# Issuing the samples' state and value-row loads from SyncE instead of GpSimd

## The chip, the cores and the metric

The kernel runs on one core of a Trainium2 chip. The metric is the device time in microseconds of one execution, from launch to the last output. Times of a kernel are given as the median of several runs. A profiled execution has a span, from its first to its last recorded instruction, and a time of its own that is a little longer.

In the text PE is TensorE, DVE is VectorE, ACT is ScalarE, POOL is GpSimd and SP is SyncE. L1077 is line 1077 of the kernel.

## What is computed

The reference is one inference step of a decoder layer with three parallel token mixers, for a prompt of 256 tokens and for 8 samples of one token each. Cut to what matters here:

```python
z = h @ w_in                                   # (tokens, 15376), split into the branches' inputs
# A: gMLP spatial gating   B: HGRN2, 8 heads of 128 x 128   C: GLA, 4 heads of 128 x 256
S_t = diag(f_t) @ S_{t-1} + outer(k_t, v_t)    # B and C, per head
o_t = S_t.T @ q_t
merged = sum(sigmoid(z_gate[n]) * (branch[n] @ w_branch[n]) for n in range(3))
x = x + gt1 * rmsnorm(merged @ w_out)
x = x + gt2 * rmsnorm(relu(h2 @ w_mlp_up) ** 2 @ w_mlp_down)
```

The prompt starts from zero states. Each sample has states of its own, given as inputs (`state_hgrn`, `state_gla`), and returns them after one update: the old state is scaled by f per row, and the outer product of the sample's k and v is added. All weights are float32.

## The kernel before

All weight matrices are streamed through PE in items of 512 KB. For each item SP issues a load into one of four `raw` buffers (L616, or L609 in the first stage). ACT then rounds the item to its high part `whi` (L109), DVE takes the difference as its low part `wlo` (L106), half an item at a time, and PE multiplies three products, whi by the high part of the activations (L659), whi by their low part (L660) and wlo by their high part (L661). `Stream.ahead` issues loads five items ahead (`LOAD_AHEAD`) and splits two items ahead (`SPLIT_AHEAD`). Six half-item buffers hold `whi` and `wlo`. Each call of `linear` runs the items of 256 output columns, and after every item it calls `background`, which moves all other work on by a little.

That other work is written as Python generators. `mixer_r` does the prompts' part of one group of four heads, `samples_r` the samples' part. There are three groups: two of HGRN2 (128 x 128 states) and one of GLA (128 x 256 states). The samples' part goes in steps of 256 KB of states: for HGRN2 one sample with its four heads is a step, 8 steps for a group; for GLA two heads of a sample, 16 steps. So there are 32 steps in all. For each step:

- `fetch` loads the step's states from the input into one of four `st` buffers (`ST_BUFS`), L1077;
- `values` loads the step's value rows, broadcast to all 128 partitions, into one of two `vbc` buffers (`VB_BUFS`), L1083. The rows come from a small DRAM tensor `vs_d` that `mixer_r` wrote before (L1134);
- ACT scales the states in place by f (L1103), DVE adds k times the row (L1105), one instruction for each head;
- the new states are stored to the output by POOL (L1106);
- later `slot` has PE multiply all states of a sample with its q (L686), and the result is gathered on DVE.

The states are fetched two steps ahead and the rows one step ahead. A fetch is made only when at most one state buffer still waits for PE (L1096), and a step's update comes three calls of `background` after its fetch (`FETCHED`). An `st` buffer comes free when PE has read it and its store is done, a `vbc` buffer when DVE has made the updates of its step.

The order of the instructions on an engine is set in one of two ways. Within a `manual_schedule` block the listed engines run in program order. All other engines are ordered by the scheduler, which puts an instruction where its inputs and buffers are ready by its own estimate, earlier program lines first. From L969 to L1404, which holds all of the samples' work, the listed engines are PE and POOL. SP, ACT and DVE are ordered by the scheduler there. In the first stage (up to L844) SP too runs in program order. Whatever its origin, the order is fixed when the program is built: on the chip an engine takes its instructions one after the other, and one that waits holds up all that stand behind it.

POOL's order around the samples' work is therefore, for each step n: the state load of step n+2 (L1077), the row load of step n+1 (L1083), the store of step n (L1106). SP has the weight items and the loads of `w_ada` (L339), which the adaLN modulation needs.

Of the kernel before, what the change touches and what calls it, by code (L numbers as in the profile page):

```python
# [15 lines left out]
P = 128  # L16
# [41 lines left out]
def hybrid_step_kernel(  # L58
# [8 lines left out]
    nc = tc.nc  # L67
# [18 lines left out]
    def blk(shape=None, dt=F32):  # L86
        shape = shape or [P, 4, NT]
        return blkp.tile(shape, dt, tag="b", name=nm("b"))
# [4 lines left out]
    def tmp(shape, tag, bufs=2):  # L93
        return tp.tile(shape, F32, tag=tag, name=nm(tag), bufs=bufs)
# [4 lines left out]
    def mul(o, a, b):  # L99
        V.tensor_tensor(o, a, b, op=ALU.mult)  # L100
# [106 lines left out]
    def rstd_small(ms, scale, out):  # L207

        n, w = out.shape
        xx, aa = tmp([P, 16], "sx")[0:n, 0:w], tmp([P, 16], "sa")[0:n, 0:w]  # L210
        c = 0
        for m in ms if isinstance(ms, list) else [ms]:
            V.tensor_scalar(xx[:, c:c + m.shape[1]], m, scale, EPS, ALU.mult, ALU.add)
            c += m.shape[1]
        V.tensor_scalar(out.bitcast(I32), xx.bitcast(I32), -0.5, 1597463007.0, ALU.mult, ALU.add)
        for _ in range(3):
            mul(aa, out, out)
            V.scalar_tensor_tensor(aa, aa, -0.5, xx, ALU.mult, ALU.mult)
            V.scalar_tensor_tensor(out, aa, 1.5, out, ALU.add, ALU.mult)
# [768 lines left out]
    vs_d = dp.tile([3, 8 * NS, P], F32, tag="vs_d", name="vs_d")  # L988
# [73 lines left out]
    def samples_r(G):  # L1062

        dv = G.dv
        nj, nh = dv // P, 512 // dv
        q, k, g = G.q, G.k, G.g
        fs = tmp([P, 4, NS], "fs")
        S.activation(fs, g[:, :, NP:NT], AF.Exp)
        qm = blk([P, 4, NS, 32])
        mul(qm, q[:, :, NP:NT].unsqueeze(3).to_broadcast([P, 4, NS, 32]),  # L1070
            delta.rearrange("p (b c) -> p b c", b=NS).unsqueeze(1).to_broadcast([P, 4, NS, 32]))
        steps = [(b, h) for b in range(NS) for h in range(0, 4, nh)]
        ahead, vals = [], []

        def fetch(b, h):
            st = tmp([P, nh, dv], "st", ST_BUFS)
            nc.gpsimd.dma_start(st, G.s_in(b, h, nh))  # L1077
            ahead.append((st, now[0]))

        def values(b, h):  # L1080
            v = tmp([P, 4, P], "vbc", VB_BUFS)
            r0 = 4 * nj * b + h * nj
            nc.gpsimd.dma_start(v, vs_d[G.i, r0:r0 + 4, :].partition_broadcast(P))  # L1083
            vals.append((v.rearrange("p (h j) v -> p h (j v)", h=nh), now[0]))

        for s in steps[0:2]:
            fetch(*s)
            yield
        values(*steps[0])
        yield  # L1090
        os_ = tmp([P, dv], f"os{G.i}", 1)
        sts = []
        for n, (b, h0) in enumerate(steps):
            if n + 2 < len(steps):

                yield lambda: len(sts) + sum(len(x[3]) for x in samples) <= ST_BUFS - 3  # L1096
                fetch(*steps[n + 2])
            if n + 1 < len(steps):
                values(*steps[n + 1])
            yield lambda: now[0] >= max(ahead[0][1] + FETCHED, vals[0][1] + FETCHED - 1)  # L1100
            st, v = ahead.pop(0)[0], vals.pop(0)[0]
            for i in range(nh):
                S.activation(st[:, i, :], st[:, i, :], AF.Copy, scale=fs[:, h0 + i, b:b + 1])  # L1103
            for i in range(nh):
                V.scalar_tensor_tensor(st[:, i, :], v[:, i, :], k[:, h0 + i, NP + b:NP + b + 1], st[:, i, :], ALU.mult, ALU.add)  # L1105
            nc.gpsimd.dma_start(G.s_out(b, h0, nh), st)  # L1106
            sts.append(st)
            if h0 + nh == 4:
                samples.append((now[0], (G, qm, os_), b, sts))
                sts = []  # L1110
            yield
        yield lambda: not samples
        yield READY
        ss, rr = tmp([P, 1], "sss", 1), tmp([P, 1], "srr", 1)
        S.activation(tmp([P, dv], "vt"), os_, AF.Square, accum_out=ss)
        rstd_small(ss, 1.0 / dv, rr)
        S.activation(os_, os_, AF.Copy, scale=rr)
        G.os = os_
        yield
# [641 lines left out]
```

## Time and profile before

| | |
|---|---|
| median of 3 runs | 1835.34 us (1832.19 to 1837.56) |
| profiled execution, its own time | 1832.18 us |
| its span | 1830.4 us |
| mean granted clock of PE | 0.997 |
| DMA, mean over the span | 242 GB/s |

The page gives the busy time of each engine, the span in slices, the chain that ended last and the costliest groups of instructions. Further views are of one stretch alone: the busy time of each engine in it, who waited for whom in it, and the instructions of one engine in order of time. In the last the columns are start, duration, engine, line, operation, written and read tile, count, and in brackets the idle time before it and what ended it. In a group's row the count is followed by the busy time and the mean duration in ns, then by the idle time of the engine before these instructions. In a waits row the numbers are microseconds in total, times, and the longest. A DMA row ends with the size of one transfer and the median time from issue to landing.

### The profile page before, as it was taken

The page shows a single profiled execution, that of the slowest core. Times are in us where ns is not written, and L with a number is a line of the kernel's source. Part 1 is how long each engine was busy: PE and PEld are TensorE (multiplying, and loading weights), DVE is VectorE, ACT ScalarE, POOL GpSimd, SP SyncE. Part 2 cuts the span into 40 slices and gives each one's busy share as a digit, 9 for nine tenths or more (in the row PEclk, how much of TensorE's full clock was granted, in tenths as well). Part 3 has the DMA queues.
Part 4 walks back from the last instruction along what each step waited for, and adds up shares of the span by engine and source line. Part 5 has one row for each costly group of instructions (what it writes and reads, how often), then busy time and mean ns, then how long its engine had stood idle before and what let it go on. Part 6 is the DMA issues. An engine that isn't in the chain of part 4 may idle for free.

```text
span 1830.4 us, 42186 instructions
## 1 busy us (share of the span) xinstructions
PE 1788.7 (98%) x17012; PEld 1696.5 (93%) x17012; DVE 1181.8 (65%) x2092; ACT 1000.3 (55%) x1818; POOL 131.3 (7%) x210
## 2 busy tenths in 40 slices
PE   6999999999999999999999999999999999999998
PEld 4889999989988999989999989999999999999997
DVE  4566677787576696566555667555666666666666
ACT  5544364666755765654445666555554545454544
POOL 4221000111111101210000000000000000000000
PEclk9999999999999999999999999999999999999999
DMA  9999697788787788897987964777666666666663
GB/s 326 354 343 304 195 304 231 215 266 276 239 287 233 229 270 278 274 323 250 308 254 265 327 180 146 246 256 227 191 197 194 197 194 196 195 195 196 196 196 106
DMA packets 330179, 442.05 MB, mean 242 GB/s; under 512 B 14946, under 2 KB 276944, under 8 KB 329984
## 3 DMA queue, kind: packets, MB, share of 16 engines
q1 hardware_dynamic: 311728, 380.26, 65.0%
q0 software_dynamic: 17184, 57.85, 9.1%
q8 instruction: 133, 2.18, 0.5%
q10 hardware_dynamic: 1072, 1.25, 0.2%
q14 instruction: 62, 0.51, 0.1%
HBM read 427.60 MB, written 11.70 MB: 240 GB/s over the span
## 4 chain that ended last, share of the span: by engine, by line
PE 88%; DMA 2%; DVE 2%; issue 1%; ACT 1%; POOL 0%; DVEq 0%; ACTq 0%; POOLq 0%
PE mm L659 27%; PE mm L661 26%; PE mm L660 26%; PE ada L376 3%; DMA vbc<-vs_d 1%; PE ada L308 1%; DVE wlo L106 1%; PE sm L851 1%; PE sm L1208 1%; PE sm L679 1%; PE sm L686 1%; DMA raw<-in_w_in_dram 0%; DVE b L106 0%; PE sm L1578 0%; ACT whi L109 0%
## 5 line engine op out<-in xcount | busy, mean ns | idle before, releaser
L659 PE MATMUL mm<-b,whi 128*128 128x264 f32 x4624 | 1292.4, 279 | 12.3 <-issue 5.1
L661 PE MATMUL mm<-b,wlo 128*128 128x264 f32 x4624 | 1279.7, 277 | 5.1 <-DVE wlo L106 4.5
L660 PE MATMUL mm<-b,whi 128*128 128x264 f32 x4624 | 1278.8, 277 | 0.8 <-DVE b L106 0.7
L106 DVE TENSOR_TENSOR wlo<-raw,whi 128x512 fp32r<-128x512 f32 x1136 | 774.4, 689 | 489.1 <-ACT whi L109 475.0
L109 ACT CAST whi<-raw 128x512 fp32r<-128x512 f32 x1136 | 691.8, 616 | 644.5 <-DVE wlo L106 331.7
L659 PEld LDWEIGHTS mm<-b,whi 128*128 128x128 f32 x4624 | 875.8, 189 | 53.0 <-issue 28.0
L661 PEld LDWEIGHTS mm<-b,wlo 128*128 128x128 f32 x4624 | 876.2, 189 | 7.3 <-DVE wlo L106 7.2
L660 PEld LDWEIGHTS mm<-b,whi 128*128 128x128 f32 x4624 | 876.2, 189 | 4.4 <-issue 3.0
L103 DVE TENSOR_TENSOR b<-b,mm 128x528 f32<-128x528 f32 (+1 forms) x137 | 95.7, 699 | 24.5 <-PE mm L661 13.0
L1105 DVE SCALAR_TENSOR_TENSOR st<-vbc,b,st 128x128 f32<-128x128 f32 (+1 forms) x96 | 34.2, 390 | 55.2 <-DMA vbc<-vs_d 50.4
L1103 ACT ACTIVATE st<-st,fs 128x128 f32<-128x128 f32 (+1 forms) x96 | 37.1, 430 | 50.5 <-DMA st<-in_state_hgrn_dram 26.9
L488 POOL DMA_DIRECT2D b<-in_w_ada_dram x64 | 46.2, 724 | 126.0 <-PE ada L308 94.4
L376 PE MATMUL ada<-araw,cT 128*32 128x512 f32 x296 | 39.8, 601 | 0.0
L308 PE MATMUL ada<-b,cT 128*32 128x256 f32 (+1 forms) x640 | 35.1, 356 | 2.8 <-DMA b<-in_w_ada_dram 2.6
L100 DVE TENSOR_TENSOR b<-b,b 128x512 f32<-128x512 f32 (+1 forms) x47 | 33.9, 741 | 1.3 <-ACT b L1221 1.0
L1106 POOL DMA_DIRECT2D out_dram<-st x32 | 23.6, 736 | 130.5 <-DVE st L1105 130.5
L308 PEld LDWEIGHTS ada<-b,cT 128*32 128x32 f32 x640 | 17.8, 113 | 14.9 <-DMA b<-in_w_ada_dram 6.2
L376 PE MATMUL ada<-b,cT 128*32 128x512 f32 x216 | 26.2, 594 | 0.0
L106 DVE TENSOR_TENSOR b<-gt,b 128x528 fp32r<-128x528 f32 x32 | 22.7, 710 | 3.2
L106 DVE TENSOR_TENSOR b<-b 128x1024 f32<-128x1024 f32 (+1 forms) x24 | 24.3, 1017 | 0.0
L1632 ACT ACTIVATE b<-vt 128x528 fp32r<-128x528 f32 x32 | 23.0, 719 | 1.0
L106 DVE TENSOR_TENSOR b<-b,b 128x1056 fp32r<-128x1056 f32 (+3 forms) x21 | 20.8, 991 | 4.0 <-ACT b L109 3.8
(344 smaller groups left out, 854.0 us busy)
## 6 DMA issues: line engine op xcount, KB each, us to landing
raw<-in_w_in_dram SPq DMA_DIRECT2D x231, 512.0 KB, 4.8
raw<-in_w_mlp_up_dram SPq DMA_DIRECT2D x128, 512.0 KB, 3.9
raw<-in_w_mlp_down_dram SPq DMA_DIRECT2D x128, 512.0 KB, 3.7
araw<-in_w_ada_dram SPq DMA_DIRECT2D x74, 512.0 KB, 5.7
b<-in_w_ada_dram SPq DMA_DIRECT2D x54, 512.0 KB, 6.6
b<-in_w_ada_dram POOLq DMA_DIRECT2D x48, 512.0 KB, 8.9
raw<-in_w_branch_dram SPq DMA_DIRECT2D x48, 512.0 KB, 4.5
raw<-in_w_out_dram SPq DMA_DIRECT2D x32, 512.0 KB, 5.3
```

What stands on the lines that cost most here:

```text
L100: V.tensor_tensor(o, a, b, op=ALU.mult)
L103: V.tensor_tensor(o, a, b, op=ALU.add)
L106: V.tensor_tensor(o, a, b, op=ALU.subtract)
L109: S.copy(hi, src)
L308: T.matmul(acc[32 * j:32 * j + 32, 0:n], cT[:, k, :], w[:, n * j:n * j + n], start=k == 0, stop=k == KT - 1)
L376: T.matmul(self.acc[32 * j:32 * j + 32, :], cT[:, k, :], ws[j // 2][:, j % 2 * 512:j % 2 * 512 + 512], start=k == 0, stop=k == KT - 1)
L488: queue.dma_start(w[:, i], w1[k * P:(k + 1) * P, :, self.k0 * P:(self.k0 + self.n) * P])
L659: T.matmul(o, a, xh(k + j), start=first and j == 0, stop=False)
L660: T.matmul(o, a, xl(k + j), start=False, stop=False)
L661: T.matmul(o, b, xh(k + j), start=False, stop=last and j == n - 1)
L1103: S.activation(st[:, i, :], st[:, i, :], AF.Copy, scale=fs[:, h0 + i, b:b + 1])
L1105: V.scalar_tensor_tensor(st[:, i, :], v[:, i, :], k[:, h0 + i, NP + b:NP + b + 1], st[:, i, :], ALU.mult, ALU.add)
```

## The change

The two loads of the samples' part are issued by SP. They use the same buffers, sources and consumers as before; the stores of the new states (L1106) and the write of `vs_d` (L1134) remain on POOL.

```diff
         def fetch(b, h):
             st = tmp([P, nh, dv], "st", ST_BUFS)
-            nc.gpsimd.dma_start(st, G.s_in(b, h, nh))
+            nc.sync.dma_start(st, G.s_in(b, h, nh))
             ahead.append((st, now[0]))
 
         def values(b, h):
             v = tmp([P, 4, P], "vbc", VB_BUFS)
             r0 = 4 * nj * b + h * nj
-            nc.gpsimd.dma_start(v, vs_d[G.i, r0:r0 + 4, :].partition_broadcast(P))
+            nc.sync.dma_start(v, vs_d[G.i, r0:r0 + 4, :].partition_broadcast(P))
             vals.append((v.rearrange("p (h j) v -> p h (j v)", h=nh), now[0]))
```

## The prediction

> **What bounds the kernel now.** I read the page's busy shares first, then one window for each part of the program, then who waited for whom where the moved loads run.
>
> ```profile
> span 1830.4 us, 42186 instructions
> PE 1788.7 (98%) x17012; PEld 1696.5 (93%) x17012; DVE 1181.8 (65%) x2092; ACT 1000.3 (55%) x1818; POOL 131.3 (7%) x210
> ...
> 0.00:350.00 350.00, 329.20 (x3139) 299.41 (x3140) 228.14 (x449) 168.97 (x288) 53.81 (x85) 1.00 0.85 289
> 350.00:830.00 480.00, 469.42 (x5152) 435.71 (x5151) 335.44 (x634) 312.45 (x637) 70.31 (x106) 0.99 0.81 266
> 830.00:1830.40 1000.40, 990.07 (x8726) 961.35 (x8724) 618.18 (x1010) 518.92 (x895) 7.17 (x19) 1.00 0.68 213
> ```
>
> TensorE sets the time. In a window row the columns are length, then busy time of PE, PEld, DVE, ACT and POOL, then clock, DMA share and GB/s. The moved loads belong to 350 to 830 us, where PE is busy 469.42 of 480.00 us: it loses 10.6 us there, and no better placing of these loads can win more than that in their own stretch. The waits of that stretch say what the 10.6 us are:
>
> ```profile
> PE mm L659 <- issue: 5.1, 2, 2.9
> PE mm L661 <- DVE wlo L106: 4.3, 5, 2.3
> PE mm L659 <- ACT whi L109: 0.3, 1, 0.3
> ...
> DVE st L1105 <- DMA vbc<-vs_d: 50.4, 19, 7.4
> ...
> ACT st L1103 <- DMA st<-in_state_hgrn_dram: 26.9, 7, 7.2
> ...
> ACT st L1103 <- DMA st<-in_state_gla_dram: 16.9, 9, 3.5
> ...
> POOL st L1077 <- PE sm L686: 153.4, 11, 30.4
> POOL out_dram L1106 <- DVE st L1105: 130.5, 17, 28.2
> ```
>
> 4.3 + 0.3 = 4.6 us of PE's loss is a wait for split weights (whi, wlo), which ScalarE and VectorE make; 5.1 us has no releaser that the profile knows. VectorE stands 50.4 us, 19 times, before the state update of line 1105 until a value row (vbc) lands, and everything behind it on VectorE, the splits too, stands with it. Why the rows are late is in GpSimd's order. First GpSimd, then VectorE, at one such place:
>
> ```profile
> 764.50 0.71 POOL L1106 DMA_DIRECT2D out_dram<-st  x1 [3.52 <-DVE st L1105]
> 773.71 0.72 POOL L1077 DMA_DIRECT2D st<-in_state_gla_dram  x1 [8.49 <-PE sm L686]
> 774.43 0.57 POOL L1083 DMA_DIRECT2D vbc<-vs_d  x1
> ...
> 763.73 0.48 DVE L1105 SCALAR_TENSOR_TENSOR st<-vbc,b,st 128x256 f32<-128x256 f32 x1
> ...
> 781.87 0.88 DVE L1105 SCALAR_TENSOR_TENSOR st<-vbc,b,st 128x256 f32<-128x256 f32 x2 [7.36 <-DMA vbc<-vs_d]
> ```
>
> There are two vbc buffers. The one that is loaded at 774.43 was free when the update two steps earlier ended, at 763.73 + 0.48 = 764.2. The load went out 10.2 us later, because in program order it stands behind a state load that waits until PE has read a state buffer (8.49 us here). VectorE then waited 7.36 us.
>
> **The change, part by part.** 32 state loads and 32 row loads, 256 KB each, leave GpSimd's queue for SyncE's. Data, buffers and consumers stay.
>
> ```profile
> L1083 POOL DMA_DIRECT2D vbc<-vs_d x32 | 18.0, 561 | 1.4 <-DMA vs_d<-sqs 1.1 <-issue 0.3
> L1077 POOL DMA_DIRECT2D st<-in_state_hgrn_dram x16 | 12.1, 758 | 99.9 <-PE sm L686 99.1 <-issue 0.8
> L1077 POOL DMA_DIRECT2D st<-in_state_gla_dram x16 | 11.9, 745 | 54.2 <-PE sm L686 54.2
> ...
> L616 SPq DMA_DIRECT2D raw<-in_w_in_dram x104: 367/368/384, 354.2 to 829.2; - x104
> L616 SPq DMA_DIRECT2D raw<-in_w_branch_dram x32: 367/368/379, 406.2 to 790.0; - x32
> ...
> SPq L616 <- DVE wlo L106: 259.4, 101, 9.0
> ...
> vbc<-vs_d POOLq DMA_DIRECT2D x32, 256.0 KB, 6.5
> ```
>
> *Issue time.* Removed from GpSimd: 18.0 + 12.1 + 11.9 = 42.0 us, on an engine that is 7% busy and sets nothing: 0. Added to SyncE: 64 issues at the 0.368 us of a weight load, 23.6 us. SyncE waits 259.4 us in this stretch for freed weight buffers alone, which covers it: 0; without that cover each issue would push the next weight load by 0.37 us.
>
> *Order of the row loads.* GpSimd's order is written out by hand in this section, SyncE's is not: the scheduler puts an instruction where its inputs and its buffer are free by its own estimate. So a row load should follow the update that frees its buffer and no longer the state load. In the place above it would go out at 764.2 and, with the row loads' median landing of 6.5 us, be there at 770.7; VectorE comes for it at 781.87 - 7.36 = 774.5. How such a wait reaches PE:
>
> ```profile
> 519.78 0.61 DVE L1105 SCALAR_TENSOR_TENSOR st<-vbc,b,st 128x128 f32<-128x128 f32 x2 [6.05 <-DMA vbc<-vs_d]
> ...
> 520.00:530.00 10.00, 8.56 (x66) 7.58 (x66) 10.00 (x17) 5.67 (x13) 0.00 (x0) 1.00 0.62 217
> ```
>
> VectorE idles 6.05 us until 519.78, then is busy for the whole next 10 us, in which PE loses 1.4. I take this part to remove the 4.6 us that PE waits for splits. Bounds: 0, if VectorE then waits at the same places for the states; 10.6 us, if the 5.1 us without a releaser go too.
>
> *State loads.* Their gate is PE's read of the buffer. GpSimd issues them as soon as that comes, and SyncE can't be earlier. The landing may change:
>
> ```profile
> b<-in_w_ada_dram SPq DMA_DIRECT2D x16, 256.0 KB, 5.2
> b<-in_w_ada_dram POOLq DMA_DIRECT2D x16, 256.0 KB, 8.2
> ...
> st<-in_state_hgrn_dram POOLq DMA_DIRECT2D x16, 256.0 KB, 5.8
> ```
>
> The only pair of equal size, the 256 KB pieces of w_ada, lands in 5.2 us from SyncE and 8.2 us from GpSimd, but in different stages. For the states I take 5 to 6 us, no change.
>
> *The first four states, and the first stage.* The first group's four st buffers are free from the start and its states are kernel inputs, so nothing holds these loads back once GpSimd's order doesn't. That such an instruction runs far ahead of its place is in GpSimd's own first microsecond:
>
> ```profile
> 0.73 0.20 POOL L878 MEMSET srow<- 128x128 f32 x1 [0.29 <-POOLq L1747]
> ...
> 35.00:75.00 40.00, 36.60 (x404) 34.78 (x404) 17.84 (x32) 23.38 (x45) 14.01 (x20) 1.00 1.03 402
> ```
>
> Line 878 stands behind the whole first stage, and it ran at 0.73 us. If the four loads are taken between the first weight loads, 4 x 256 KB = 1.05 MB enter a stage whose DMA is full (share 1.03, 402 GB/s) while PE is short of work (36.60 of 40.00 us): 1.05 MB / 402 GB/s = 2.6 us. Bounds 0 (taken later, or PE's slack absorbs it) and 2.6; I take the middle, 1.3.
>
> *SyncE's queue.* What stands behind a waiting state load is weight loads. Program and scheduler place it where PE's read should come, and the weight loads behind it wait for splits that follow PE too, so I take 0. The price if that fails is the second rival.
>
> *Sum.* The profiled execution took 1832.18 us. Less 4.6, plus 1.3: 1828.9. The median of the three runs, 1835.34, stands 3.2 us above that execution; in its terms the forecast is **1832.0 us**. Three runs spread over 5.4 us (1832.19 to 1837.56), so 0.3%, 5.5 us, is about what can be told from no change: the forecast is a small gain that a measurement can't tell from none.
>
> **The rivals.** *Nothing reaches PE.* The row wait goes, the wait for states takes its place (ACT's 26.9 + 16.9 = 43.8 us remain, and VectorE can't update what ScalarE hasn't scaled), and only the early loads cost: +1.3, 1836.6. For it: 50.4 us of VectorE's waits give only 4.6 us on PE even now. Against: the loss at 520 us came right behind a row wait. The Trainium skill, "DMA: Bandwidth & Descriptors", section "Issuing engines are not separate DMA queues", speaks for this rival: it says that issuing from several engines saves only the time of issuing, since all share the same 16 DMA engines. The 42.0 us of issue that leave GpSimd agree with it in that they lie on no path; it leaves out the order within a queue, which is what I count on.
>
> *All of the loss goes.* The two pauses without a releaser (5.1 us) come where state and row loads leave GpSimd in one burst; spread out, they vanish as well, and PE's slack hides the early loads: -10.6, 1824.7. Against: nothing in the trace ties those pauses to the loads.
>
> *SyncE stands at a state load (slower).* The scheduler's order is fixed beforehand. Where it puts a state load earlier than PE really frees the buffer, all weight loads behind it wait. GpSimd's waits for PE at these loads are the measure: 153.4 us in 11 waits, the longest 30.4. How long may SyncE stand?
>
> ```profile
> 588.55 0.75 POOL L1077 DMA_DIRECT2D st<-in_state_hgrn_dram  x1 [17.09 <-PE sm L686]
> ...
> 610.00:620.00 10.00, 10.00 (x91) 10.00 (x90) 5.69 (x17) 6.47 (x19) 0.00 (x0) 1.00 0.65 216
> ...
> L659 PE MATMUL mm<-b,whi 128*128 128x264 f32 x1090 | 308.7, 283 | 5.3 <-issue 5.1 <-ACT whi L109 0.3
> L106 DVE TENSOR_TENSOR wlo<-raw,whi 128x512 fp32r<-128x512 f32 x273 | 182.0, 685 | 66.4 <-ACT whi L109 64.4 <-PE sm L686 1.3
> ...
> DMA to landing us min/median/max: 3.4/4.7/11.5
> ```
>
> An undisturbed 10 us holds 91 matmuls. The 104 + 32 = 136 weight loads of the stretch feed 3 x 1090 matmuls, 24 each, so one load lasts PE 2.6 us. Loads run five ahead, 13.2 us; less the 4.7 us that a weight load takes to land and 2 x 0.685 us for its two halves on VectorE, 7.1 us are left before PE starves. From a stand of 7.1 us on it decides. One stand like the 17.09 us above costs 10.0 us, with the early loads 11.3 and no gain: 1846.6 (the longest, 30.4 us, would give 1859.9). For it: GpSimd had such waits, and nothing passes a waiting load on SyncE. Against: SyncE's own 101 waits for splits follow PE too, so the weight load behind a state load is seldom due long before PE's read.
>
> *In line behind weights (slower).* On SyncE's queue a state or a row lies behind a weight load already issued: 0.524 MB at 266 GB/s is 1.97 us for each of 64 loads, 126 us more of waiting on ACT and DVE at worst. By today's ratio of PE's 10.6 us to the 94.2 us (50.4 + 43.8) of these waits, 0.11, that is 14 us; half of the loads so met: +7, with the early loads +8.3, 1843.6. Against: 5.2 us of the w_ada pieces on SyncE's queue, among its weight loads. The Trainium skill, same page, section "SWDGE vs HWDGE vs iDMA", has the rule behind this: the software and hardware paths feed different internal queues of each DMA engine, which takes turns between them, so the move gives up a queue of its own. No run here shows the turns.
>
> **How the numbers follow.** Forecast 0.30, nothing reaches PE 0.06, all goes 0.29, SyncE stands 0.26, in line 0.09. The forecast and the first rival lie within 0.3%: same 0.36. Faster 0.29, slower 0.26 + 0.09 = 0.35. The forecast alone runs from -4.6 to +1.3, 1830.7 to 1836.6. Both signs hold much of the chance, so the range of 8 in 10 takes in the rivals on either side, each at its own price: 1822 to 1847; the stand of 30.4 us is left out.
>
> **What would show it.** Row loads at SyncE right behind the update that frees the buffer, and VectorE's 50.4 us of row waits down to under 15: the order is right. PE's loss in 350 to 830 us down from 10.6 to about 6: the size is right; unchanged, the first rival. Four state loads before 100 us and PE's busy time in 35 to 75 us below 36.6: the early loads. Weight loads that wait for PE's read of a state by 7 us or more, and ACT short of weights: SyncE stands. State landings of 8 us: in line. The forecast is wrong if the median moves by more than 5.5 us either way.

## The result, and the profile after

| | before | after |
|---|---|---|
| median | 1833.96 us (5 runs, 1832.19 to 1837.56) | 1840.81 us (5 runs, 1839.72 to 1843.00) |
| ratio to before, 95% interval | | 1.0038 [1.0024, 1.0052] |
| profiled execution, its own time | 1832.18 us | 1839.72 us |
| its span | 1830.4 us | 1837.9 us |

The changed kernel is 0.38% slower, and the interval leaves no change out. The forecast was 1832.0 us, no difference that can be told. First the page of the changed kernel (span and busy times), then its windows, with the columns as before.

```profile
span 1837.9 us, 42199 instructions
PE 1787.0 (97%) x17012; PEld 1697.6 (92%) x17012; DVE 1183.5 (64%) x2092; ACT 1000.6 (54%) x1818; POOL 90.2 (5%) x146
```

```profile
0.00:350.00 350.00, 319.15 (x3055) 292.17 (x3056) 221.92 (x440) 164.69 (x279) 53.78 (x85) 0.98 0.85 286
350.00:830.00 480.00, 470.60 (x5173) 436.92 (x5172) 338.81 (x638) 312.61 (x636) 29.21 (x42) 0.99 0.81 263
830.00:1837.90 1007.90, 997.25 (x8790) 968.56 (x8788) 622.77 (x1017) 523.34 (x903) 7.18 (x19) 1.00 0.69 214
...
35.00:75.00 40.00, 25.59 (x297) 24.17 (x296) 11.41 (x22) 16.60 (x31) 12.86 (x18) 0.87 1.01 376
```

PE's idle time is 1837.9 - 1787.0 = 50.9 us, before 1830.4 - 1788.7 = 41.7, so 9.2 us more; PE's busy time is 1.7 us less, and 9.2 - 1.7 = 7.5 us is the whole difference of the spans. By windows, PE lost 329.20 - 319.15 = 10.0 us in the first 350 us, a stretch that runs no sample's step, won 470.60 - 469.42 = 1.2 us in the stretch of the moved loads, and lost 0.3 us behind it. The loss sits in 35 to 75 us: 36.60 us busy before, 25.59 after. The granted clock in that stretch is 0.87, where it was 1.00 before.

Two views tell what PE waited for there: its waits in the first 350 us, and ScalarE's order around the longest of them.

```profile
PE mm L659 <- ACT b L825: 14.4, 4, 12.2
```

```profile
56.20 0.60 ACT L825 COPY b<-mm 128x528 f32<-128x528 f32 x1 [1.25 <-PE mm L661]
69.49 1.14 ACT L109 CAST whi<-raw 128x512 fp32r<-128x512 f32 x2 [12.70 <-DMA raw<-in_w_in_dram]
```

The profile books one wait of 12.2 us to ScalarE's copy (b), but that copy had ended at 56.8. What came last was a weight item: ScalarE stood 12.70 us before it could split one, at 69.49. SyncE's order, which issues the items, and the group of its state loads in that stretch:

```profile
39.71 8.31 SPq L1077 DMA_DIRECT2D st<-in_state_hgrn_dram  x3
48.12 5.47 SPq L616 DMA_DIRECT2D raw<-in_w_in_dram  x1
53.63 2.55 SPq L1077 DMA_DIRECT2D st<-in_state_hgrn_dram  x1
56.29 34.23 SPq L616 DMA_DIRECT2D raw<-in_w_in_dram  x10
```

```profile
L1077 SPq DMA_DIRECT2D st<-in_state_hgrn_dram x4: 462/1740/6827, 39.7 to 53.6; - x4
...
DMA to landing us min/median/max: 16.6/20.3/27.0
```

The first group's four state loads did run ahead of their place, between the weight loads of the first stage, and they landed after 16.6 to 27.0 us, where the 256 KB of a state took 5.8 us before. The weight item issued between them, at 48.12, landed 21.3 us later, at 69.4: it is the one that ScalarE stood for. Why so long, and why the weights with them, is in the DMA queues. q0 carries GpSimd's transfers (here the pieces of w_ada, 1.71 MB / 470 = 3.6 KB a packet), q1 SyncE's. The columns are packets, MB and the share of 16 engines' time; before and after, each in 55 to 60 us.

```profile
q0 software_dynamic: 371, 1.33, 65.1%
q1 hardware_dynamic: 374, 0.73, 37.6%
```

```profile
q0 software_dynamic: 470, 1.71, 87.2%
q1 hardware_dynamic: 469, 0.23, 16.0%
```

In these 5 us both queues move about the same number of packets, whatever their size: 371 and 374 before, 470 and 469 after. Before, a packet of q1 was some 2 KB of weights (0.73 MB / 374). After, it is about 500 bytes (0.23 MB / 469), since a state row of one head is 128 floats. So SyncE's queue, which alone brings the weight items, fell from 0.73 to 0.23 MB in 5 us, while w_ada's pieces ran ahead faster than before (1.71 MB), and all weight items behind the states stood in this line. From 50 to 65 us q1 moved 0.26 + 0.23 + 0.23 = 0.72 MB, where 0.73 in 5 us would be 2.2 MB. Just after 65 us the queued pieces of w_ada were through, and q1 ran free (1.50 MB in the next 5 us).

In the stretch of the moved loads (350 to 830 us) these are the waits of PE, ScalarE, VectorE and SyncE, and then the landings:

```profile
PE mm L660 <- issue: 2.5, 1, 2.5
PE sm L1249 <- ACT b L1252: 2.2, 1, 2.2
PE mm L659 <- issue: 2.0, 1, 2.0
PE mm L659 <- ACT whi L109: 1.2, 1, 1.2
PE mm L661 <- DVE wlo L106: 1.1, 2, 0.8
...
DVE st L1105 <- ACT st L1103: 25.3, 10, 5.0
...
ACT st L1103 <- DMA st<-in_state_gla_dram: 21.2, 8, 5.2
...
ACT st L1103 <- DMA st<-in_state_hgrn_dram: 12.2, 5, 6.7
...
DVE st L1105 <- DMA vbc<-vs_d: 8.7, 4, 3.8
...
SPq L1077 <- PE sm L686: 9.5, 7, 3.8
```

```profile
vbc<-vs_d SPq DMA_DIRECT2D x32, 256.0 KB, 4.9
st<-in_state_gla_dram SPq DMA_DIRECT2D x16, 256.0 KB, 5.9
st<-in_state_hgrn_dram SPq DMA_DIRECT2D x12, 256.0 KB, 5.6
```

The row waits went as forecast, 50.4 to 8.7 us. In their place VectorE waits 25.3 us for the states that ScalarE scales, and ScalarE 21.2 + 12.2 = 33.4 us for their loads. PE's waits for splits fell from 4.6 to 2.3 us, the pauses without a releaser from 5.1 to 4.5, and a new wait of 2.2 us (L1249) took back most of the gain.

### The profile page after: what moved, and what is told of

The parts are those of the page before. It is cut to its first block, busy times and chain, and to the rows that moved or that the text cites. A ratio compares the mean times of both kernels' runs of the same rounds, so it can differ in the third digit from the quotient of the medians.

```text
span 1837.9 us, 42199 instructions
## 1 busy us (share of the span) xinstructions
PE 1787.0 (97%) x17012; PEld 1697.6 (92%) x17012; DVE 1183.5 (64%) x2092; ACT 1000.6 (54%) x1818; POOL 90.2 (5%) x146
## 4 chain that ended last, share of the span: by engine, by line
PE 89%; DMA 2%; DVE 2%; ACT 1%; issue 1%; DVEq 0%; ACTq 0%; SPq 0%
PE mm L659 27%; PE mm L660 27%; PE mm L661 27%; PE ada L376 3%; DMA st<-in_state_gla_dram 1%; PE ada L308 1%; PE sm L851 1%; DVE wlo L106 1%; PE sm L679 1%; PE sm L1208 1%; PE sm L686 0%; DMA raw<-in_w_in_dram 0%; ACT whi L109 0%; PE sm L1578 0%; DMA vbc<-vs_d 0%
## 5 line engine op out<-in xcount | busy, mean ns | idle before, releaser
L1105 DVE SCALAR_TENSOR_TENSOR st<-vbc,b,st 128x128 f32<-128x128 f32 (+1 forms) x96 | 33.9, 392 | 34.1 <-ACT st L1103 25.3
L1103 ACT ACTIVATE st<-st,fs 128x128 f32<-128x128 f32 (+1 forms) x96 | 36.3, 429 | 33.7 <-DMA st<-in_state_gla_dram 21.2
L1106 POOL DMA_DIRECT2D out_dram<-st x32 | 23.7, 741 | 301.0 <-DVE st L1105 266.7
```

## The experiments

Each ran beside the kernel before, whose median was 1834.18 us beside the first four (up to the rows alone) and 1834.44 us beside the last four (from the states alone on); a ratio is to that, with its 95% interval. All diffs are against the changed kernel.

**The first four state loads back on GpSimd.** Only these four of the 64 moved loads are put back.

```diff
-            nc.sync.dma_start(st, G.s_in(b, h, nh))
+            early = G.i == 0 and b < 4
+            (nc.gpsimd if early else nc.sync).dma_start(st, G.s_in(b, h, nh))
```

> The first group's first four state loads go back to GpSimd, which holds them in program order; the other 28 state loads and all 32 row loads stay on SyncE. Theory (early loads: four state loads of 512-byte packets take turns, packet by packet, with the 4096-byte packets of w_ada in the first stage and starve the weights): PE's busy time in the first 350 us returns from 319.2 to about 329, and the time falls by some 10 us from the changed kernel's 1840.8, to about 1831. Rival (the order of SyncE, VectorE and ScalarE in 350 to 830 us costs the time): stays at 1838 to 1841.

Measured: 1832.74 us, ratio 0.9990 [0.9981, 0.9999]. Its window of the first 350 us:

```profile
0.00:350.00 350.00, 329.93 (x3123) 300.43 (x3124) 226.84 (x447) 167.17 (x284) 53.93 (x85) 0.99 0.85 287
```

The first 350 us are back at 329.93 us of PE, and with them the whole loss: four transfers of 64 made it. The other 60 are worth 0.1%, and the interval just reaches to nothing.

**The first four held on SyncE.** They keep their queue, but a one-element copy into the buffer ties each of them to `fs`, which is ready only when the prompts' part of the group has run. It separates when they are issued from who issues them.

```diff
+            if G.i == 0 and b < 4:
+                V.tensor_copy(st[:, 0, 0:1], fs[:, 0, 0:1])
             nc.sync.dma_start(st, G.s_in(b, h, nh))
```

> All loads stay on SyncE, but VectorE first copies one column of fs into each of the first group's first four state buffers, so that their loads can't go out before fs is there (about 365 us). Four small copies are added. Theory (when, not which queue): as with the loads on GpSimd, about 1831, no state load before 350 us, PE's wait of 12.2 us at 57 us gone. Rival (SyncE's queue itself is what costs): 1838 or more.

Measured: 1831.43 us, ratio 0.9994 [0.9984, 1.0004]. Its windows and the group of its HGRN2 state loads:

```profile
0.00:350.00 350.00, 330.32 (x3131) 300.70 (x3132) 227.77 (x448) 168.17 (x287) 53.93 (x85) 0.99 0.85 288
350.00:830.00 480.00, 469.64 (x5175) 436.45 (x5174) 339.68 (x641) 314.79 (x638) 29.29 (x42) 1.00 0.82 267
```

```profile
L1079 SPq DMA_DIRECT2D st<-in_state_hgrn_dram x16: 367/457/1431, 375.3 to 587.2; - x16
```

All 16 now start after 375 us, and the loss is gone with all 64 loads on SyncE. So it is the place in time, not the issuing engine in itself.

**The four early loads in packets of 2 KB.** They stay on SyncE among the first-stage weights. The same 1.05 MB is read as rows of 512 floats, so the four heads' rows come to other partitions, and the first four samples' states are not the reference's.

```diff
+            src = G.s_in(b, h, nh)
+            if G.i == 0 and b < 4:
+                src = state_hgrn[0, b, 0:4].rearrange("h (p r) v -> (h p) (r v)", r=4).rearrange("p (h v) -> p h v", h=4)
-            nc.sync.dma_start(st, G.s_in(b, h, nh))
+            nc.sync.dma_start(st, src)
```

> The first group's first four state loads read the same 256 KB as 128 pieces of 2048 bytes instead of 512 pieces of 512 bytes (the states so come in another arrangement, and four samples' HGRN2 results of that group differ from the reference). Still on SyncE, still early. Theory (turns packet by packet): the four loads are 512 packets instead of 2048; at the 465 packets that SyncE's queue gets in 5 us they take 5.5 us instead of 22, so PE's 12.2 us wait shrinks to 0 to 4 us and the time falls to 1831 to 1835. Rival (the 1.05 MB themselves in a full stage, 2.6 us of DMA time, and the place in the queue): the wait stays near 12 us, 1840.

Measured: 1833.43 us, ratio 0.9997 [0.9987, 1.0007]. The group of the four loads, PE's wait, the first window, and the queues in 55 to 60 us:

```profile
L1080 SPq DMA_DIRECT2D st<-in_state_hgrn_dram x4: 457/474/491, 40.3 to 44.0; - x4
```

```profile
PE mm L659 <- ACT b L825: 6.9, 5, 4.2
```

```profile
0.00:350.00 350.00, 326.93 (x3097) 298.29 (x3098) 226.40 (x445) 166.16 (x281) 53.93 (x85) 0.99 0.85 287
```

```profile
q0 software_dynamic: 363, 1.33, 66.1%
q1 hardware_dynamic: 366, 0.69, 36.3%
```

Queue and bytes are those of the changed kernel, the loads start at nearly the same time (40.3 us, there 39.7), and PE's wait falls from 12.2 to 4.2 us, the ratio from 1.0038 to 0.9997: packet size is the larger part of the loss. What is left in this window, 329.20 - 326.93 = 2.3 us, is near the 2.6 us that bytes alone were given, but it can't be read so closely: the rows alone (below), with no early load, have 327.42 us there. In the changed kernel one of the four issues also held SyncE for 6.8 us, here none for over 0.5. No run parts that stand of SyncE from the turns of the queue.

**Only the rows moved, only the states moved.** One edit each: the state loads of the changed kernel put back, or the row loads put back.

```diff
-            nc.sync.dma_start(st, G.s_in(b, h, nh))
+            nc.gpsimd.dma_start(st, G.s_in(b, h, nh))
```

> Only the 32 row loads go to SyncE, all state loads stay on GpSimd as before the change. Theory: no early loads, so no loss in the first stage; the row loads go out when their buffer is free, VectorE's row waits of 50.4 us fall below 15, and PE gains in 350 to 830 us what it gained with the whole change (1.2 us) up to 4.6: 1829 to 1833 where the kernel before has 1834. Rival (row loads on SyncE delay weight loads): slower than before, 1836 or more.

```diff
-            nc.sync.dma_start(v, vs_d[G.i, r0:r0 + 4, :].partition_broadcast(P))
+            nc.gpsimd.dma_start(v, vs_d[G.i, r0:r0 + 4, :].partition_broadcast(P))
```

> Only the 32 state loads go to SyncE, the row loads stay on GpSimd as before the change. Theory (early state loads in turns with w_ada): the four early loads are there, so PE waits some 12 us at 57 us and the time is 1840 to 1845. Rival (it needs the row loads too): 1834 to 1836.

Measured: rows alone 1832.97 us, ratio 0.9994 [0.9985, 1.0003]; states alone 1858.01 us, ratio 1.0123 [1.0104, 1.0142]. First the window of the rows alone, then PE's longest wait and the window of the states alone:

```profile
350.00:830.00 480.00, 470.46 (x5162) 436.59 (x5161) 338.70 (x635) 312.39 (x637) 52.94 (x74) 0.99 0.82 266
```

```profile
PE mm L659 <- ACT b L825: 14.4, 4, 11.9
```

```profile
350.00:830.00 480.00, 459.96 (x5028) 425.93 (x5027) 325.13 (x605) 301.75 (x613) 45.28 (x72) 0.98 0.79 252
```

The rows alone bring VectorE's row waits down to 9.0 us and give PE 470.46 - 469.42 = 1.0 us of the 4.6 forecast. The states alone bring the early wait, but 1840 to 1845 us was too little: 10.6 us more (470.60 - 459.96) go in 350 to 830 us.

**States alone, the first four held.** The edit of the held kernel on top of the one above, to part the two losses.

> State loads on SyncE with the first four held until fs is there, row loads on GpSimd. Row loads on GpSimd no longer stand behind state loads that wait for PE, only behind the stores. If the gain of the held kernel (about 1831.4 against 1834.2 before) comes from the row loads' queue, this kernel is at 1833 to 1835; if it comes from parting the row loads from the state loads, whichever moves, 1831 to 1833.

Measured: 1848.67 us, ratio 1.0077 [1.0063, 1.0091], so the expectation failed. Its windows, and the longest of PE's waits in 350 to 830 us:

```profile
0.00:350.00 350.00, 329.22 (x3123) 299.18 (x3124) 227.04 (x447) 167.57 (x284) 53.80 (x85) 0.99 0.84 287
350.00:830.00 480.00, 457.79 (x5014) 423.31 (x5013) 327.62 (x616) 305.37 (x624) 46.70 (x74) 0.99 0.81 259
```

```profile
PE mm L659 <- issue: 6.9, 2, 4.5
PE mm L661 <- DVE wlo L106: 4.2, 4, 3.1
PE mm L659 <- ACT whi L109: 3.8, 1, 3.8
```

The first stage is whole again (329.22), and the second loss stays: 457.79 us of PE against 469.64 with all loads on SyncE and the same four held. These rows hold 14.9 us, where pauses without a releaser and splits have 6.8 in the changed kernel. What makes the splits late and the pauses long here stays open. Neither the changed kernel nor before has the loads parted in this way.

**Two of the four held.** Only samples 2 and 3 are tied to `fs`; 0.52 MB go early, in small packets.

```diff
+            if G.i == 0 and 2 <= b < 4:
+                V.tensor_copy(st[:, 0, 0:1], fs[:, 0, 0:1])
```

> As the changed kernel, but only two of the first group's state loads stay early; the third and fourth are held until fs is there. Theory (packets on SyncE's queue set the loss): 1024 packets of 512 bytes instead of 2048, 11 us of turns instead of 22, so about half of the loss: PE's longest wait 4 to 7 us, time 1834 to 1837. Rival (a single early load is enough to break the stage): near 1840.

Measured: 1840.37 us, ratio 1.0036 [1.0024, 1.0048], slower than the theory's 1834 to 1837. PE's wait, and SyncE's queue in 55 to 60 us:

```profile
PE mm L659 <- ACT b L825: 12.8, 4, 9.4
```

```profile
q1 hardware_dynamic: 469, 0.23, 15.9%
```

Half the packets gave 9.4 of 12.2 us, not half, and a time that can't be told from that of all four (ratio 1.0038). That is the figure of the rival in the expectation, by which a single early load is enough; no run has one alone, so it isn't ruled out. Another reading that fits, but that no run tests by itself: 0.52 MB at 0.23 MB in 5 us is 11 us, and 1.05 MB would be 23 us, but w_ada's pieces end at about 65 us and what is left then runs free. By this reading the wait goes with the time that the small packets hold the queue while another queue is full, not with their number.

**The four early loads from ScalarE.** They go early and in small packets, but on a queue of their own (q10), and 11 to 18 us earlier than in the changed kernel. The copy from `A1`, ready in the first stage, sets when they are issued.

```diff
+            early = G.i == 0 and b < 4
+            if early:
+                V.tensor_copy(st[:, 0, 0:1], A1[:, 0, 0:1])
-            nc.sync.dma_start(st, G.s_in(b, h, nh))
+            (nc.scalar if early else nc.sync).dma_start(st, G.s_in(b, h, nh))
```

> The first four state loads stay early and of 512-byte packets, but are issued by ScalarE, on a queue of their own, after a small copy that waits for the first A1 (about 30 us). Theory (queues take turns packet by packet): three queues share, so the weights on SyncE's queue get 2048 of about 6.6 KB a turn instead of 2048 of about 6.1, and no state packets stand between them: PE's long wait is gone or under 4 us, time 1831 to 1835. Rival (early 512-byte loads slow all DMA, on whatever queue): 1838 or more. The four issues on ScalarE may cost 1 to 2 us in either case.

Measured: 1830.75 us, ratio 0.9982 [0.9971, 0.9992]. The group of the four loads, PE's wait, and the queues in 40 to 45 us:

```profile
L1080 ACTq DMA_DIRECT2D st<-in_state_hgrn_dram x4: 374/383/403, 28.5 to 35.8; - x4
```

```profile
PE mm L659 <- ACT b L825: 6.1, 6, 1.7
```

```profile
q0 software_dynamic: 345, 1.12, 57.4%
q1 hardware_dynamic: 345, 0.66, 35.3%
q10 hardware_dynamic: 346, 0.17, 11.6%
```

Three queues, 345, 345 and 346 packets. The weights keep 0.66 MB in these 5 us (0.73 before): the small packets now have turns of their own, which are short, and no longer take those of the weights. No wait at these copies is over 1.7 us.

Two things limit what this run shows. It changes the time along with the queue: half of q10's 2112 packets had passed by 35 us, and from 30 to 33 us the weights' queue moved 6 packets in all. And the first stage isn't whole. GpSimd's first write of `vs_d` (L1134, here L1137) needs the first group's value rows and so marks how late that group is. In this order: before, the changed kernel, the 2 KB packets, and the loads from ScalarE.

```profile
L1134 POOL DMA_DIRECT2D vs_d<-sqs x3: 508/529/557, 357.3 to 637.8; - x3
L1134 POOL DMA_DIRECT2D vs_d<-sqs x3: 507/529/557, 367.0 to 644.5; - x3
L1137 POOL DMA_DIRECT2D vs_d<-sqs x3: 510/532/560, 362.0 to 636.6; - x3
L1137 POOL DMA_DIRECT2D vs_d<-sqs x3: 507/532/560, 361.8 to 636.5; - x3
```

The first write is 9.7 us late in the changed kernel and still 4.7 and 4.5 us late in the last two. By the last write these two are 1.2 and 1.3 us ahead of before, and the changed kernel is 6.7 us late. So the early loads cost the first stage some 4.5 us even in large packets or on another queue, and that comes back before 637 us, which is why the time shows no cost. What gives it back, no run tests. Besides the kernel with the first four on GpSimd this is the only version whose interval lies below 1; from the held one (1831.43) it can't be told.

## Why the prediction was wrong

**The first four states, and the first stage.** This is the step that failed. Its mechanism was right: the four loads ran ahead to 39.7 to 53.6 us, and PE's busy time in 35 to 75 us fell below 36.6. Its size was wrong: 1.3 us, with an upper bound of 2.6, for a measured 10.0 us of PE's busy time (9.7 us by the first write of `vs_d`). The step divided bytes by the rate of all queues together, 402 GB/s, as if the states took their share from everyone. They took it from the weights alone: with 512-byte packets on SyncE's queue the engines still gave q1 every second packet, so that it carried 0.23 instead of 0.73 MB in 5 us. With packets of the weights' size PE's busy time is 2.3 us short, within the bound, though that write is 4.7 us late.

**Order of the row loads.** The order came as said, and so did the row waits, 50.4 to 8.7 us, under 15. The 4.6 us for PE were mis-sized: 1.2 us after, 1.0 with the rows alone. Over all kernels here with the rows on SyncE PE's busy time in that window runs from 468.57 to 472.96 us, 0.9 less to 3.5 more than before, so the gain isn't known closely; none reaches 4.6. For this part the first rival, in which nothing reaches PE, was nearly right: VectorE then waits for the states at the same updates.

**State loads.** Landings of 5.6 and 5.9 us on SyncE after 350 us: no change, right. The four early ones, 20.3 us in the median, were in a stretch for which the only price taken, 5.8 us, didn't hold.

**Issue time and SyncE's queue.** Taken at 0. In 350 to 830 us SyncE's longest stand at a state load is 3.8 us, short of the 7.1 from which the second slower case was to begin, and PE's split waits shrank: right. That rival, which was given 0.26, didn't occur. In the first stage the issues did take time, 1.7 us in the median and 6.8 at most, where 0.368 was taken.

**In line behind weights.** The rival with 0.09 was priced in 350 to 830 us, where row and state landings (4.9 to 5.9 us) show no line. But the rule that stood beside it decided the first stage. The Trainium skill, "DMA: Bandwidth & Descriptors", section "SWDGE vs HWDGE vs iDMA", says that the two paths feed different queues of an engine, which takes turns, and that it switches at packet boundaries. The trace agrees: 470 and 469 packets in 5 us. It was the other way round from the rival: weights stood behind states. The prediction says that no run shows the turns, but the profile before did, in 371 and 374 packets; the first-stage term could have been worked out from them.

**The sum** in terms of the profiled executions: forecast 1828.9, measured 1839.72, 10.8 us apart. The early loads account for 10.0 - 1.3 = 8.7, the rows for 4.6 - 1.2 = 3.4, the rest of the program for 0.3, less 1.7 us by which PE's busy time is shorter: 10.7. The median moved by 1840.81 - 1833.96 = 6.9 us, more than the 5.5 from which the prediction called itself wrong. It still lies within the range of 1822 to 1847, but by luck: the range reached so high for the two slower rivals, and neither occurred.

## What to carry to other kernels

When a load moves to an engine whose order the scheduler makes, ask first how early it can run, and what shares the queue there. Look at the size of its packets, not only at its bytes: on the full DMA engines here each queue got equal packets, so small packets on the queue that feeds the bound engine starved it. Held until their time, or issued still earlier on a queue of their own, they cost no time that could be measured. The loss didn't go with the number of packets: half of them cost as much time as all. A wait removed from an engine that isn't the bound was worth little here, since the next wait at the same instruction took most of its place.

## What the runs showed of the hardware

Equal packets for each queue, not equal bytes, hold for two queues (371 and 374; 470 and 469) and for three (345, 345, 346), in stretches in which all of them were moving loads. Where one has little to move they don't hold: in 30 to 35 us of the last kernel it is 256 for GpSimd's queue, 206 for SyncE's and 891 for ScalarE's. A third queue, from ScalarE, gave small packets a place where they took little from the weights: 0.66 MB in 5 us, against 0.23 when they lay on the weights' own queue.
